# Split weight panels kept in DRAM and loaded back, and two PSUM banks that go through a panel half by half

## The chip, the cores and the metric

The kernel runs on one NeuronCore of a Trainium2 chip, in one launch. The metric is the device time of that launch in microseconds (us); lower is better. Three runs of the kernel before took 3841.34, 3851.86 and 3855.9 us; their median, 3851.86 us, is the time to compare with.

## The reference, cut to what matters

Two sequences go through one layer: a prompt of 256 tokens and a sample of 2048, each token a row of 1024 numbers. All arithmetic is float32.

```python
h = _rmsnorm(x, prm['norm_mix'][l])
p = h @ prm['w_in'][l]                     # 1024 -> 3504 columns
...                                        # three token mixers: GLA, RWKV-7, SSD, each in both directions
mix = jnp.concatenate([o_gla, o_rwkv, o_ssd], axis=-1)
x = x + mix @ prm['w_out'][l]              # 1024 -> 1024
h = _rmsnorm(x, prm['norm_ffn'][l])
x = x + (jax.nn.silu(h @ prm['ffn_gate'][l]) * (h @ prm['ffn_up'][l])) @ prm['ffn_down'][l]   # 2816 wide
```

The four projections are the dense work. `w_in` is used for 5 groups of tokens (the prompt's 256 and four times 512 of the sample), `w_out` for 9 blocks of 256 tokens, and the FFN weights for the same 5 groups.

## The kernel before, in words

**Split products.** A float32 product is made of three matmuls in the float32r form: each operand is the sum of a rounded part (hi) and the rest (lo), and hi times hi, hi times lo and lo times hi are added up in one PSUM bank (`acc3`, line 372: for every 128 rows k of the weights three matmuls). The activations are split when they are made (tiles `hT`, `mix`, and `b9`, `b9x`, the slots of the FFN's inner activations).

**Panels.** Weights come in panels of 256 columns (`panel`, line 281). A panel of 1024 rows has two halves of four k-blocks. For each pair of k-blocks a raw tile `wr` of 256 KB is loaded on SyncE's queue (line 293; 4 buffers, one whole panel), ScalarE copies it to `wh`, which rounds it (line 295), and VectorE subtracts to get `wl` (line 296; in the input projection GpSimd does every second of these). `wh` and `wl` have two buffers of one half each. So a panel costs four loads, four ScalarE copies and four subtractions each time it is used, and a half can be filled only after the matmuls have left the half that lay in its buffer. A panel has two outputs of 24 matmuls or, for 512 tokens with the tokens as output rows, four: in `in_chan` (line 382) and the FFN's gate and up two outputs of 128 columns by 512 tokens, in `tok` (line 395: `in_tok`, `out_proj`) two or four outputs of 128 tokens by 256 columns. Each output goes through both halves before the next begins, so the first half of the panel is left when three quarters of it are done (with four outputs, seven eighths), the second half at its end.

**PSUM.** Dense outputs take turns on the two banks of pool `d`; in the sample's output projection and the FFN (`dense(wide=True)`, line 144) a third one, `g`, joins them. `evac` (line 378) copies an output to a tile `ev`, on ScalarE and VectorE in turn.

**Stages.** Passes over the sequence interleave mixers and dense work. First the prompt's input projection (14 panels), then that of the sample's four groups (11, 14, 14, 14 panels, and at the end the 3 panels that the first group had left out: `in_gates`, line 439), each beside the forward mixers of the blocks before (`pass_a`, line 967). Then backwards: for each block of 256 tokens the backward mixers (`pass_b`, line 978) and the output projection (`out_proj`, line 1023, 4 panels), interleaved with the FFN of the groups already done (`ffn`, line 1039). The last group's FFN runs alone. The prompt's output projection comes early, beside the second group of the sample.

**Order.** The framework orders each engine's instructions before the run, by the order in the program, with priorities and by a simulated time line; each engine then works through its own list and waits on semaphores. A DMA is issued by the queue of its engine in that order too: SyncE's queue has the loads of panels, most of the mixers' loads and the stores of `ev`; ScalarE's the mixers' stores. An instruction that waits holds up all that stands behind it on its engine.

Of the kernel before, what the change touches and what calls it, by code (L numbers as in the profile page):

```python
# [8 lines left out]
F32 = mybir.dt.float32  # L9
F32R = mybir.dt.float32r  # L10
# [8 lines left out]
P = 128  # L19
# [50 lines left out]
class Encoder:  # L70
    def __init__(self, ctx, tc, ins, y_prompt, y_sample):
        self.ctx, self.tc, self.nc, self.ins = ctx, tc, tc.nc, ins
        self.Lp, self.Ls = ins["x_prompt"].shape[1], ins["x_sample"].shape[1]
        self.NT = self.Lp + self.Ls
        self.NB = self.NT // TB
        self.yp, self.ys = y_prompt, y_sample
        self.flip, self.free, self.turn = 0, False, 0
        pool = lambda n, b, **k: ctx.enter_context(tc.tile_pool(name=n, bufs=b, **k))
        self.cp = pool("const", 1)
        self.wp = pool("weights", 2)  # L80
        self.hp = pool("dense", 1)
# [33 lines left out]
    def mm(self, out, lhsT, rhs, start=True, stop=True, tp=None, lax=False):  # L115
        self.nc.tensor.matmul(out, lhsT=lhsT, rhs=rhs, start=start, stop=stop, tile_position=tp, skip_group_check=lax)  # L116

    SLOT = {"av0": "b9", "av1": "b9x", "acc0": "b4a", "acc1": "b4b", "acc2": "b4c", "acc3": "b4d", "gate": "b4e",
            "ga": "b4a", "gb": "b4b", "NF": "b4d", "gP": "b4e", "gqxb": "b2b", "gsq": "b2a", "gth": "b2b", "qgb": "qg", "ggt": "gv",
            "sxd": "b2b", "sth": "b2a", "qsb": "qs", "sz": "sxs", "sC": "scb", "sdr": "scb",  # L120
# [157 lines left out]
        return self.ins["x_sample"][0, t:t + P, :], self.ys[0, t:t + P, :]  # L278


    def panel(self, srcs, kt, pool=0):
        n = sum(w for _, w in srcs)
        nc, out = self.nc, []
        for k0 in range(0, kt, 4):
            kn = min(4, kt - k0)
            hi = self.wp.tile([P, 4, 256], F32R, tag="wh", name="wh", bufs=2)
            lo = self.wp.tile([P, 4, 256], F32R, tag="wl", name="wl", bufs=2)
            for j in range(0, kn, 2):
                raw = self.wp.tile([P, 2, 256], F32, tag="wr", name="wr", bufs=4)
                o = 0  # L290
                for ap, w in srcs:
                    with nc.allow_non_contiguous_dma(reason="column panel"):
                        nc.sync.dma_start(out=raw[:, :, o:o + w], in_=ap[(k0 + j) * P:(k0 + j + 2) * P, :].rearrange("(k p) n -> p k n", p=P))
                    o += w
                self.copy(hi[:, j:j + 2, :n], raw[:, :, :n], "a")
                self.tt(lo[:, j:j + 2, :n], raw[:, :, :n], hi[:, j:j + 2, :n], ALU.subtract, nc.gpsimd if j == 2 and pool else None)
            out += [(hi[:, k], lo[:, k]) for k in range(kn)]
        return out

    def inv_rms(self, x, tag):  # L300
# [68 lines left out]
    def new_hT(self):  # L369
        return [self.hp.tile([P, KD, GS], F32R, tag=f"hT{i}", name=f"hT{i}") for i in range(2)]  # L370

    def acc3(self, ps, lhs, rhs, kt):

        for k in range(kt):
            for a, b in ((0, 0), (0, 1), (1, 0)):
                self.mm(ps, lhs(k, a), rhs(k, b), start=k == 0 and a + b == 0, stop=k == kt - 1 and a == 1)

    def evac(self, out, in_):
        self.flip += 1
# [2 lines left out]
    def in_chan(self, hT, t0, n, cols, dst):  # L382

        w = self.ins["w_in"][0]
        pan = self.panel([(w[:, o:o + c], c) for o, c in cols], KD, 1)
        c0 = 0
        for dram, idx, rows in dst:
            ps = self.ps(self.dps, "d")
            self.acc3(ps[:rows, :n], lambda k, a: pan[k][a][:, c0:c0 + rows], lambda k, a: hT[a][:, k, :n], KD)
            ev = self.hp.tile([P, GS], F32, tag="ev", name="ev", bufs=3)  # L390
            self.evac(ev[:rows, :n], ps[:rows, :n])
            self.nc.sync.dma_start(out=dram[:rows, idx, t0:t0 + n], in_=ev[:rows, :n])
            c0 += rows

    def tok(self, lhs, pan, i, kt, wide=True):

        ps = self.dense(wide)
        self.acc3(ps[:, :256], lambda k, a: lhs[a][:, k, i * P:(i + 1) * P], lambda k, a: pan[k][a], kt)
        return ps[:, :256]

    def in_tok(self, hT, t0, n, off, dst, d0):
        pan = self.panel([(self.ins["w_in"][0][:, off:off + 256], 256)], KD, 1)
        for i in range(n // P):
            ps = self.tok(hT, pan, i, KD, False)
            ev = self.hp.tile([P, GS], F32, tag="ev", name="ev", bufs=3)
            self.evac(ev[:, :256], ps)
            self.nc.sync.dma_start(out=dst[t0 + i * P:t0 + (i + 1) * P, d0:d0 + 256], in_=ev[:, :256])

    def normed(self, t0, n, gain, src, rs=None):
        hT = self.new_hT()  # L410
# [612 lines left out]
    def out_proj(self, b, mix):  # L1023
        nc, t0 = self.nc, b * TB
        ss = [self.hp.tile([P, 4], F32, tag="so", name="so", bufs=4) for _ in range(2)]
        for c in range(4):
            cs = slice(256 * c, 256 * c + 256)
            pan = self.panel([(self.ins["w_out"][0][:, cs], 256)], KD)
            for i in range(2):
                x = self.hp.tile([P, 256], F32, tag="ev", name="xo", bufs=3)  # L1030
                nc.sync.dma_start(out=x[:], in_=self.xrow(t0 + i * P)[0][:, cs])
                self.tt(x[:], self.tok(mix, pan, i, KD, t0 >= self.Lp), x[:], ALU.add)
                nc.scalar.dma_start(out=self.d_x2[t0 + i * P:t0 + (i + 1) * P, cs], in_=x[:])
                self.square(ss[i], c, x[:])
        for i in range(2):
            self.rs2[t0 + i * P] = self.inv_rms4(ss[i], "rn", self.rn[:, t0 // P + i:t0 // P + i + 1])


    def ffn(self, t0, n, after=None, inside=False):
# [16 lines left out]
        for fn in [2] + [4] * ((FT - 2) // 4):  # L1056
            if not inside:
                av = [self.m([P, 4, GS], f"av{i}", F32R) for i in range(2)]
            for f in range(0, fn, 2):
                cs = slice((f0 + f) * P, (f0 + f + 2) * P)  # L1060
                if inside:
                    gate = self.hp.tile([P, 2, n], F32, tag="ev", name="gate", bufs=3)
                else:
                    gate = self.m([P, 2, GS], "gate")
                for name in ("ffn_gate", "ffn_up"):
                    pan = self.panel([(ins[name][0][:, cs], 256)], KD)
                    for j in range(2):
                        ps = self.dense(not inside)
                        self.acc3(ps[:, :n], lambda k, a: pan[k][a][:, j * P:(j + 1) * P], lambda k, a: hT[a][:, k, :n], KD)
                        if name == "ffn_gate":  # L1070
                            self.act(gate[:, j, :n], ps[:, :n], AF.Tanh, scale=0.5)
                            self.stt(gate[:, j, :n], gate[:, j, :n], 1.0, ps[:, :n], ALU.add, ALU.mult)
                        else:
                            self.stt(gate[:, j, :n], ps[:, :n], 0.5, gate[:, j, :n], ALU.mult, ALU.mult)
                            self.copy(av[0][:, f + j, :n], gate[:, j, :n], "a")
                            self.tt(av[1][:, f + j, :n], gate[:, j, :n], av[0][:, f + j, :n], ALU.subtract)
            for c in range(4):
                half = None
                if f0 + fn == FT and after and c < after[1] // P:
                    with self.tc.high_priority(offset=3000):  # L1080
                        t = after[0] + c * P
                        ready = self.ready.get(after[0]) or self.ready.setdefault(after[0], self.new_hT())
                        half = self.norm_T(self.d_x2[t:t + P, :], g, ready, c, self.rs2[t])
                cs = slice(256 * c, 256 * c + 256)
                pan = self.panel([(ins["ffn_down"][0][f0 * P:(f0 + fn) * P, cs], 256)], fn)
                for i in range(nt):
                    self.tt(acc[i][:, c], self.tok(av, pan, i, fn, not inside), acc[i][:, c], ALU.add)
# [121 lines left out]
```

## Time and profile before

| | |
|---|---|
| median of three runs | 3851.86 us |
| profiled execution | 3852.02 us |
| its span, first to last instruction | 3850.2 us |
| TensorE busy | 3607.3 us, 94% |
| VectorE busy | 2453.1 us, 64% |
| ScalarE busy | 1459.3 us, 38% |
| GpSimd busy | 560.5 us, 15% |
| mean granted TensorE clock | 0.963 of 2.4 GHz |
| DMA | 486.5 MB, 126 GB/s |

PE is TensorE's matmul side, PEld its weight loads, DVE VectorE, ACT ScalarE, POOL GpSimd, SP SyncE (a queue of DMAs here). A matmul's duration overlaps that of the next one, so that a busy PE need not be at its peak: what a stream of matmuls costs is the distance of their starts. L116 is line 116 of the kernel. The chain that ended last is followed back from the last instruction, at each step to what released it or to the instruction before it on its engine.

### The profile page before, as it was taken

The numbers are of one execution on the slowest core, as the hardware profiler recorded it, in microseconds if no ns is written. First come the engines' busy times: TensorE is split into PE (matmuls) and PEld (weight loads), VectorE is DVE, ScalarE is ACT, GpSimd is POOL, SyncE is SP. The second block draws the span as 40 slices with busy tenths as digits, with TensorE's granted clock in tenths as the row PEclk, the third lists the DMA queues.
The fourth block names the chain that finished last, engine by engine and source line by source line (L and its number), as shares of the span: only waits on it lengthen the run. The fifth ranks groups of instructions, "written<-read, shape, count | busy, mean of one in ns | idle before, by whom it ended". The sixth has DMA issues, their size and how long they took to land.

```text
span 3850.2 us, 75004 instructions
## 1 busy us (share of the span) xinstructions
PE 3607.3 (94%) x29534; PEld 3022.0 (78%) x29534; DVE 2453.1 (64%) x5551; ACT 1459.3 (38%) x3228; POOL 560.5 (15%) x564
## 2 busy tenths in 40 slices
PE   6898889899989879899989999999999999999998
PEld 6777676667767667788878888888888888888887
DVE  5943486784893788876766565565654765645444
ACT  4533244544453455443432323323233332333222
POOL 2321113332332333110000000000000000000000
PEclk9899899999989988998999999999999999999999
DMA  6444242434324423455543434434343442434232
GB/s 177 157 140 123 88 149 96 126 98 134 124 92 127 134 94 112 150 165 162 169 151 122 128 119 131 135 128 136 102 146 103 146 131 83 147 105 137 93 99 93
DMA packets 430192, 486.50 MB, mean 126 GB/s; under 512 B 49344, under 2 KB 389456, under 8 KB 428688
## 3 DMA queue, kind: packets, MB, share of 16 engines
q1 hardware_dynamic: 390720, 422.40, 35.5%
q10 hardware_dynamic: 38112, 55.65, 4.1%
q8 instruction: 232, 3.80, 0.4%
q0 software_dynamic: 1008, 3.67, 0.3%
q14 instruction: 120, 0.98, 0.1%
HBM read 395.42 MB, written 86.18 MB: 125 GB/s over the span
## 4 chain that ended last, share of the span: by engine, by line
PE 75%; DVE 13%; DMA 6%; ACT 3%; issue 2%; POOL 0%; ACTq 0%; SPq 0%; DVEq 0%; POOLq 0%
PE d L116 47%; PE g L116 15%; PE s L116 5%; PE a L116 3%; PE c L116 3%; DVE mix L102 3%; DMA mix<-d_xb 1%; DVE wl L92 1%; DMA x<-d_x 1%; DVE mix L92 1%; PE d L362 1%; DVE x L102 1%; DMA b<-d_rk 1%; DMA x<-in_x_sample 1%; ACT wh L109 0%
## 5 line engine op out<-in xcount | busy, mean ns | idle before, releaser
L116 PE MATMUL d<-hT,wh 128*128 128x512 f32 (+3 forms) x4384 | 1272.5, 374 | 12.8 <-ACT wh L109 4.6
L109 ACT ACTIVATE wh<-wr 128x512 fp32r<-128x512 f32 (+1 forms) x1084 | 624.6, 621 | 987.2 <-PE d L116 573.1
L116 PEld LDWEIGHTS d<-hT,wh 128*128 128x128 f32 (+1 forms) x4384 | 788.9, 191 | 162.5 <-issue 10.2
L92 DVE TENSOR_TENSOR wl<-wr,wh 128x512 fp32r<-128x512 f32 x944 | 651.8, 718 | 338.0 <-ACT wh L109 322.9
L116 PE MATMUL d<-hT,wl 128*128 128x512 f32 (+2 forms) x2192 | 811.9, 374 | 24.3 <-DVE wl L92 24.1
L116 PEld LDWEIGHTS d<-hT,wl 128*128 128x128 f32 (+1 forms) x2192 | 416.9, 191 | 103.6 <-DVE wl L92 29.1
L116 PE MATMUL g<-hT,wh 128*128 128x512 f32 x896 | 285.1, 394 | 0.1
L116 PE MATMUL d<-wh,hT 128*128 128x256 f32 x1216 | 259.0, 303 | 14.6 <-ACT wh L109 8.2
L116 PE MATMUL d<-wh,b 128*128 128x256 f32 x928 | 266.3, 289 | 4.7 <-DVE b4d L92 3.2
L92 POOL TENSOR_TENSOR wl<-wr,wh 128x512 fp32r<-128x512 f32 (+1 forms) x140 | 198.3, 1420 | 485.6 <-ACT wh L109 365.7
L116 PE MATMUL d<-wl,b 128*128 128x256 f32 x928 | 260.2, 282 | 0.0
L116 PE MATMUL d<-wh,b9x 128*128 128x256 f32 x928 | 257.9, 281 | 0.0
L116 PEld LDWEIGHTS d<-wh,hT 128*128 128x128 f32 x1216 | 206.3, 202 | 26.5 <-ACT wh L109 10.0
L116 PEld LDWEIGHTS g<-hT,wh 128*128 128x128 f32 x896 | 166.6, 188 | 35.3 <-issue 0.7
L116 PE MATMUL d<-wl,hT 128*128 128x256 f32 x608 | 182.5, 302 | 9.5 <-DVE wl L92 9.5
L116 PEld LDWEIGHTS d<-wh,b 128*128 128x128 f32 x928 | 174.1, 188 | 12.3 <-DVE b4d L92 3.6
L116 PE MATMUL d<-wh,mix 128*128 128x256 f32 x832 | 168.8, 292 | 8.3 <-ACT mix L109 5.5
L116 PE MATMUL g<-hT,wl 128*128 128x512 f32 x448 | 175.5, 392 | 0.0
L116 PEld LDWEIGHTS d<-wl,b 128*128 128x128 f32 x928 | 174.7, 189 | 0.7 <-issue 0.3
L116 PEld LDWEIGHTS d<-wh,b9x 128*128 128x128 f32 x928 | 174.5, 189 | 0.5
L102 DVE SCALAR_TENSOR_TENSOR mix<-mix,cwh,mix 128x256 f32<-128x256 f32 x288 | 140.3, 539 | 18.3 <-ACT mix L105 18.2
L116 PEld LDWEIGHTS d<-wh,mix 128*128 128x128 f32 x832 | 135.8, 195 | 11.7 <-ACT mix L109 5.8
(384 smaller groups left out, 6220.9 us busy)
## 6 DMA issues: line engine op xcount, KB each, us to landing
wr<-in_w_in SPq DMA_DIRECT2D x260, 256.0 KB, 3.4
wr<-in_ffn_gate SPq DMA_DIRECT2D x220, 256.0 KB, 2.9
wr<-in_ffn_up SPq DMA_DIRECT2D x220, 256.0 KB, 2.9
wr<-in_ffn_down SPq DMA_DIRECT2D x220, 256.0 KB, 2.8
wr<-in_w_out SPq DMA_DIRECT2D x144, 256.0 KB, 3.3
x<-in_x_sample SPq DMA_DIRECT2D x20, 512.0 KB, 3.5
x<-d_x SPq DMA_DIRECT2D x20, 512.0 KB, 3.9
q_s<-qs ACTq DMA_DIRECT2D x18, 520.0 KB, 3.1
```

Source lines behind the costliest of these rows:

```text
L92: (eng or self.nc.vector).tensor_tensor(out=out, in0=a, in1=b, op=op)
L102: (eng or self.nc.vector).scalar_tensor_tensor(out=out, in0=a, scalar=s, in1=b, op0=op0, op1=op1)
L109: self.nc.scalar.activation(out=out, in_=in_, func=AF.Copy)
L116: self.nc.tensor.matmul(out, lhsT=lhsT, rhs=rhs, start=start, stop=stop, tile_position=tp, skip_group_check=lax)
L362: self.nc.tensor.transpose(ps[:, k * P:(k + 1) * P], h[:, (4 * q + k) * P:(4 * q + k + 1) * P], self.c["ident"])
```

## The change

A panel now has a name, and the kernel counts its uses. The 14 panels of `w_in` are split as before in their first use (the prompt) and in their second; after the second, ScalarE's queue also writes the four split halves (two `wh`, two `wl`, 512 KB each) to DRAM. From the third use on no raw tile is loaded, copied or subtracted: SyncE's queue loads the split halves into `wh` and `wl`, four DMAs of 512 KB in place of four of 256 KB. For `w_out` the first use writes and the other 8 load. The FFN's panels are split at each use, as before. The two buffers of `wh` and `wl` get names of their own, and a list tells which is free first.

`acc3` now takes several outputs (`jobs`) and goes through the panel half by half: all outputs take the first half, then all take the second, so that as many PSUM banks are in use at once. With four outputs (`in_tok` with 512 tokens) the first pair takes the halves in the order 0, 1, the second pair in the order 1, 0, and the next panel's first half goes to the buffer that is free first. `ffn_down`'s panels of four k-blocks are one half, and are used one output at a time as before.

```diff
+        self.uses, self.kept, self.slots = {}, {}, [0, 1]
...
+    KEPT = {"w_in": 2, "w_out": 1}
...
-    def panel(self, srcs, kt, pool=0):
+    def panel(self, name, srcs, kt, pool=0, snake=False):
         n = sum(w for _, w in srcs)
-        nc, out = self.nc, []
+        nc, out, slots = self.nc, [], []
+        use = self.uses[name] = self.uses.get(name, 0) + 1
+        kept = self.kept.get(name)
+        keep = kept is None and use == self.KEPT.get(name[0], 0)
+        if keep:
+            kept = self.kept[name] = self.dr.tile([2, P, kt, n], F32, name=f"d_w{len(self.kept)}", tag=f"d_w{len(self.kept)}")
         for k0 in range(0, kt, 4):
             kn = min(4, kt - k0)
-            hi = self.wp.tile([P, 4, 256], F32R, tag="wh", name="wh", bufs=2)
-            lo = self.wp.tile([P, 4, 256], F32R, tag="wl", name="wl", bufs=2)
-            for j in range(0, kn, 2):
...
+            slot = self.slots.pop(0)
+            slots.append(slot)
+            hi = self.wp.tile([P, 4, 256], F32R, tag=f"wh{slot}", name="wh", bufs=1)
+            lo = self.wp.tile([P, 4, 256], F32R, tag=f"wl{slot}", name="wl", bufs=1)
+            parts = [(hi[:, :kn, :n], 0), (lo[:, :kn, :n], 1)]
+            if kept is not None and not keep:
+                for t, i in parts:
+                    nc.sync.dma_start(out=t.bitcast(F32), in_=kept[i, :, k0:k0 + kn])
+            else:
+                for j in range(0, kn, 2):
...
+                if keep:
+                    for t, i in parts:
+                        nc.scalar.dma_start(out=kept[i, :, k0:k0 + kn], in_=t.bitcast(F32))
+            out.append([(hi[:, k], lo[:, k]) for k in range(kn)])
+        self.slots += slots[::-1] if snake else slots
         return out
...
-    def acc3(self, ps, lhs, rhs, kt):
-        for k in range(kt):
-            for a, b in ((0, 0), (0, 1), (1, 0)):
-                self.mm(ps, lhs(k, a), rhs(k, b), start=k == 0 and a + b == 0, stop=k == kt - 1 and a == 1)
+    def acc3(self, jobs, pan, kt, order=(0, 1)):
+        order = order[:1] if len(pan) == 1 else order
+        for n, q in enumerate(order):
+            for ps, lhs, rhs in jobs:
+                for j, w in enumerate(pan[q]):
+                    for a, b in ((0, 0), (0, 1), (1, 0)):
+                        self.mm(ps, lhs(4 * q + j, a, w), rhs(4 * q + j, b, w), start=n == 0 and j == 0 and a + b == 0,
+                                stop=n == len(order) - 1 and j == len(pan[q]) - 1 and a == 1)
...
     def in_tok(self, hT, t0, n, off, dst, d0):
-        pan = self.panel([(self.ins["w_in"][0][:, off:off + 256], 256)], KD, 1)
-        for i in range(n // P):
-            ps = self.tok(hT, pan, i, KD, False)
...
+        pan = self.panel(("w_in", off), [(self.ins["w_in"][0][:, off:off + 256], 256)], KD, 1, snake=n == GS)
+        for i0 in range(0, n // P, 2):
+            for i, ps in enumerate(self.tok(hT, pan, (i0, i0 + 1), KD, False, (0, 1) if i0 == 0 else (1, 0)), i0):
...
-            pan = self.panel([(self.ins["w_out"][0][:, cs], 256)], KD)
-            for i in range(2):
+            pan = self.panel(("w_out", c), [(self.ins["w_out"][0][:, cs], 256)], KD)
+            for i, ps in enumerate(self.tok(mix, pan, (0, 1), KD, t0 >= self.Lp)):
...
-                self.tt(x[:], self.tok(mix, pan, i, KD, t0 >= self.Lp), x[:], ALU.add)
+                self.tt(x[:], ps, x[:], ALU.add)
...
-                    pan = self.panel([(ins[name][0][:, cs], 256)], KD)
-                    for j in range(2):
-                        ps = self.dense(not inside)
-                        self.acc3(ps[:, :n], lambda k, a: pan[k][a][:, j * P:(j + 1) * P], lambda k, a: hT[a][:, k, :n], KD)
+                    pan = self.panel((name, f0 + f), [(ins[name][0][:, cs], 256)], KD)
+                    jobs = [(self.dense(not inside)[:, :n], lambda k, a, w, j=j: w[a][:, j * P:(j + 1) * P],
+                             lambda k, a, w: hT[a][:, k, :n]) for j in range(2)]
+                    self.acc3(jobs, pan, KD)
```

## Rows read from the trace of the kernel before

**Rows 1.** The page's head: busy time of each engine.
```profile
PE 3607.3 (94%) x29534; PEld 3022.0 (78%) x29534; DVE 2453.1 (64%) x5551; ACT 1459.3 (38%) x3228; POOL 560.5 (15%) x564
```
**Rows 2.** Stages: length, busy PE, PEld, DVE, ACT, POOL, clock, DMA share, GB/s.
```profile
115.00:400.00 285.00, 261.17 (x2194) 202.50 (x2193) 161.57 (x343) 110.72 (x260) 74.97 (x68) 0.95 0.45 139
400.00:1560.00 1160.00, 1032.90 (x9098) 801.44 (x9098) 843.75 (x1844) 532.80 (x1219) 342.51 (x346) 0.92 0.36 114
1560.00:1960.00 400.00, 375.08 (x4294) 341.26 (x4292) 299.02 (x737) 167.02 (x385) 35.94 (x40) 0.96 0.54 170
1960.00:3330.00 1370.00, 1354.97 (x10509) 1158.62 (x10509) 831.65 (x1932) 442.14 (x939) 70.53 (x70) 1.00 0.39 125
```
**Rows 3.** The chain of waits by line: 400 to 1560, 1560 to 1960, 1960 to 3330.
```profile
by line: PE d L116 30.2%; DVE mix L102 7.5%; PE a L116 6.9%; PE s L116 4.6%; DMA mix<-d_xb 4.6%; issue 4.6%; PE g L116 3.6%; PE c L116 2.8%; DVE mix L92 2.0%; DVE wl L92 2.0%; DMA b<-d_rk 1.8%; DVE b L129 1.5%; ACT mix L105 1.3%; ACT b4a L1
by line: PE d L116 53.0%; PE s L116 10.9%; PE c L116 7.1%; PE g L116 5.9%; issue 2.7%; PE a L116 2.3%; DVE wl L92 1.8%; DMA sxs<-d_z 1.8%; DVE srs L102 1.1%; PE s L593 1.1%; DMA d_x<-xo 0.9%; DMA x<-d_x 0.9%; DMA b<-d_gl 0.6%; DVE b9x L92 0
by line: PE d L116 53.4%; PE g L116 25.9%; PE s L116 6.0%; PE c L116 3.3%; PE a L116 1.9%; DMA x<-d_x 1.6%; DMA qg<-q_g 1.0%; DVE wl L92 0.9%; PE d L362 0.8%; issue 0.8%; DMA wr<-in_w_out 0.6%; PE a L1019 0.4%; DMA wr<-in_ffn_gate 0.4%; PE 
```
**Rows 4.** The splits: duration ns least/median/most.
```profile
L109 ACT ACTIVATE wh<-wr x1084: 480/620/667, 14.0 to 3827.4; 128x512 fp32r<-128x512 f32 x178, 128x352 fp32r<-128x352 f32 x3
L92 DVE TENSOR_TENSOR wl<-wr,wh x944: 514/686/1796, 15.8 to 3828.2; 128x512 fp32r<-128x512 f32 x188, 128x352 fp32r<-128x352 f32 x1
L92 POOL TENSOR_TENSOR wl<-wr,wh x140: 927/1316/3867, 15.2 to 1506.1; 128x512 fp32r<-128x512 f32 x130, 128x352 fp32r<-128x352 f32 x10
```
**Rows 5.** Who waited for what: us in total, times, longest.
```profile
PE d L116 <- DVE wl L92: 33.9, 22, 4.0
PE d L116 <- ACT wh L109: 13.1, 11, 5.0
PE d L116 <- DVE ev L113: 9.6, 5, 4.0
ACT wh L109 <- PE d L116: 573.1, 258, 8.7
```
**Rows 6.** Pieces of the chain: start, us, matmuls; 512 columns, then 256.
```profile
3338.32 10.88 PE d L116 x48
2131.20 5.62 PE d L116 x46
```
**Rows 7.** Matmuls on `mix` in the first, third and last of eight sample blocks.
```profile
L116 PE MATMUL d<-wh,mix x96: 276/281/582, 1788.2 to 1820.4; 128*128 128x256 f32 x96
...
L116 PE MATMUL d<-wh,mix x96: 277/281/387, 2105.5 to 2136.5; 128*128 128x256 f32 x96
...
L116 PE MATMUL d<-wh,mix x80: 276/281/290, 3302.9 to 3327.6; 128*128 128x256 f32 x80
L116 PE MATMUL g<-wh,mix x48: 277/281/387, 3301.5 to 3327.0; 128*128 128x256 f32 x48
```
**Rows 8.** DMA issues: count, KB each, median us from issue to landing.
```profile
wr<-in_w_out SPq DMA_DIRECT2D x144, 256.0 KB, 3.3
x<-in_x_sample SPq DMA_DIRECT2D x20, 512.0 KB, 3.5
```
**Rows 9.** Four loads of 512 KB in a row: SyncE's time line, then landings.
```profile
1958.20 0.34 SPq L353 DMA_DIRECT2D x<-d_x  x1
1958.59 0.42 SPq L1054 DMA_DIRECT2D b4a<-d_x  x1
1959.11 0.38 SPq L353 DMA_DIRECT2D x<-d_x  x1
1959.54 0.42 SPq L1054 DMA_DIRECT2D b4b<-d_x  x1
...
b4a<-d_x SPq DMA_DIRECT2D x1, 512.0 KB, 4.5
b4b<-d_x SPq DMA_DIRECT2D x1, 512.0 KB, 6.2
```
**Rows 10.** ScalarE's DMA queue: packets, MB, share of 16 engines' span.
```profile
q10 hardware_dynamic: 38112, 55.65, 4.1%
```

More of the change, by code (lines that the diff above doesn't have):

```diff
@@ L284, in panel @@
         for k0 in range(0, kt, 4):
             kn = min(4, kt - k0)
-            hi = self.wp.tile([P, 4, 256], F32R, tag="wh", name="wh", bufs=2)
-            lo = self.wp.tile([P, 4, 256], F32R, tag="wl", name="wl", bufs=2)
-            for j in range(0, kn, 2):
[L289 to L296, printed above, removed]
@@ L297, in panel @@
-            out += [(hi[:, k], lo[:, k]) for k in range(kn)]
+            slot = self.slots.pop(0)
[8 more added lines that the diff above has]
+                for j in range(0, kn, 2):
+                    raw = self.wp.tile([P, 2, 256], F32, tag="wr", name="wr", bufs=4)
+                    o = 0
+                    for ap, w in srcs:
+                        with nc.allow_non_contiguous_dma(reason="column panel"):
+                            nc.sync.dma_start(out=raw[:, :, o:o + w], in_=ap[(k0 + j) * P:(k0 + j + 2) * P, :].rearrange("(k p) n -> p k n", p=P))
+                        o += w
+                    self.copy(hi[:, j:j + 2, :n], raw[:, :, :n], "a")
+                    self.tt(lo[:, j:j + 2, :n], raw[:, :, :n], hi[:, j:j + 2, :n], ALU.subtract, nc.gpsimd if j == 2 and pool else None)
+                if keep:
+                    for t, i in parts:
+                        nc.scalar.dma_start(out=kept[i, :, k0:k0 + kn], in_=t.bitcast(F32))
@@ L384, in in_chan @@
         w = self.ins["w_in"][0]
-        pan = self.panel([(w[:, o:o + c], c) for o, c in cols], KD, 1)
-        c0 = 0
+        pan = self.panel(("w_in", cols[0][0]), [(w[:, o:o + c], c) for o, c in cols], KD, 1)
+        c0, jobs = 0, []
         for dram, idx, rows in dst:
             ps = self.ps(self.dps, "d")
-            self.acc3(ps[:rows, :n], lambda k, a: pan[k][a][:, c0:c0 + rows], lambda k, a: hT[a][:, k, :n], KD)
+            jobs.append((ps[:rows, :n], lambda k, a, w, c0=c0, rows=rows: w[a][:, c0:c0 + rows], lambda k, a, w: hT[a][:, k, :n]))
+            c0 += rows
@@ L390, in in_chan @@
+        self.acc3(jobs, pan, KD)
+        for (ps, _, _), (dram, idx, rows) in zip(jobs, dst):
             ev = self.hp.tile([P, GS], F32, tag="ev", name="ev", bufs=3)
-            self.evac(ev[:rows, :n], ps[:rows, :n])
+            self.evac(ev[:rows, :n], ps)
             self.nc.sync.dma_start(out=dram[:rows, idx, t0:t0 + n], in_=ev[:rows, :n])
[L393 to L399, printed above, removed]
@@ L401, in in_tok, with tok @@
-    def in_tok(self, hT, t0, n, off, dst, d0):
-        pan = self.panel([(self.ins["w_in"][0][:, off:off + 256], 256)], KD, 1)
-        for i in range(n // P):
-            ps = self.tok(hT, pan, i, KD, False)
-            ev = self.hp.tile([P, GS], F32, tag="ev", name="ev", bufs=3)
-            self.evac(ev[:, :256], ps)
-            self.nc.sync.dma_start(out=dst[t0 + i * P:t0 + (i + 1) * P, d0:d0 + 256], in_=ev[:, :256])
+    def tok(self, lhs, pan, tiles, kt, wide=True, order=(0, 1)):
+        jobs = [(self.dense(wide)[:, :256], lambda k, a, w, i=i: lhs[a][:, k, i * P:(i + 1) * P], lambda k, a, w: w[a]) for i in tiles]
+        self.acc3(jobs, pan, kt, order)
+        return [j[0] for j in jobs]
@@ new lines, in in_tok @@
+    def in_tok(self, hT, t0, n, off, dst, d0):
+        pan = self.panel(("w_in", off), [(self.ins["w_in"][0][:, off:off + 256], 256)], KD, 1, snake=n == GS)
+        for i0 in range(0, n // P, 2):
+            for i, ps in enumerate(self.tok(hT, pan, (i0, i0 + 1), KD, False, (0, 1) if i0 == 0 else (1, 0)), i0):
+                ev = self.hp.tile([P, GS], F32, tag="ev", name="ev", bufs=3)
+                self.evac(ev[:, :256], ps)
+                self.nc.sync.dma_start(out=dst[t0 + i * P:t0 + (i + 1) * P, d0:d0 + 256], in_=ev[:, :256])
@@ L1084, in ffn @@
                 cs = slice(256 * c, 256 * c + 256)
-                pan = self.panel([(ins["ffn_down"][0][f0 * P:(f0 + fn) * P, cs], 256)], fn)
+                pan = self.panel(("ffn_down", f0, c), [(ins["ffn_down"][0][f0 * P:(f0 + fn) * P, cs], 256)], fn)
                 for i in range(nt):
-                    self.tt(acc[i][:, c], self.tok(av, pan, i, fn, not inside), acc[i][:, c], ALU.add)
+                    self.tt(acc[i][:, c], self.tok(av, pan, (i,), fn, not inside)[0], acc[i][:, c], ALU.add)
                     if f0 + fn == FT:
```

8 lines of the change are left out of this document (5 added, 3 removed).

## The prediction, made before the changed kernel was run

> **What bounds the kernel now.** I read the head of the page first: TensorE is busy 94% of the span, VectorE 64%, ScalarE 38% [rows 1]. That is an average, so the stages come next [rows 2]. In 1960 to 3330 TensorE is busy 1355 of 1370 us at full clock: little can be gained there by anything that is not TensorE's own work. In 400 to 1560, the input projection of the sample beside the forward mixers, it is busy 1033 of 1160 us at a granted clock of 0.92, with VectorE at 844 us. There the chain of waits alternates between TensorE, VectorE and the mixers' loads [rows 3]: the matmul entries in its row add up to 48%. Only then do I ask what panels cost. The subtraction of `wl` is 2.0% of that chain, 1.8% of the one from 1560 to 1960 and 0.9% of the one from 1960 to 3330 [rows 3], that is 23, 7 and 12 us. In all, dense matmuls waited 33.9 us for `wl` and 13.1 us for `wh` [rows 5]. The loads of raw tiles are early: what ScalarE's copies wait for is a buffer that TensorE has not left yet, 573 us in 258 waits [rows 5], not a DMA. So the panels' price today is some 50 us of waits, out of 3850.
>
> **What is removed.** Of 70 panels of `w_in` the last 42 are loaded split, of 36 of `w_out` the last 32. Each had four copies and four subtractions. ScalarE loses 74 x 4 = 296 copies of 0.62 us, 184 us; VectorE 84 + 128 = 212 subtractions of 0.69 us, 146 us; GpSimd 84 of 1.3 us, 110 us [rows 4]. Of this only 84 subtractions, 58 us of VectorE, and 168 copies, 104 us of ScalarE, lie in 400 to 1560, where these engines are on the path; that is 7% of what VectorE does there. The other subtractions and copies lie in the output projection, beside a full TensorE.
>
> **What is added: loads between release and use.** Before, the load was done ahead, and between the release of a half and its use stood a copy and a subtraction, 0.62 + 0.69 us for the first two k-blocks. Now the whole load stands there, two DMAs of 512 KB. A load of that size lands 3.5 us after its issue, a raw one of 256 KB after 3.3 [rows 8]. Four such loads in a row bound a pair and a whole panel: the second was issued 0.39 us after the first and landed 4.5 us later, 4.9 us in all, and the fourth landed 7.5 us after the first was issued [rows 9]. I take 4.9 us for a half. Against it stands the time in which the other half is used: 24 matmuls. With 512 columns at 10.88/48 = 0.227 us that is 5.4 us, with 256 columns at 5.62/46 = 0.122 us it is 2.9 us [rows 6].
>
> In `in_chan` 5.4 us cover 4.9. In the 9 loaded `in_tok` panels (four outputs) the first buffer is freed 24 matmuls, 2.9 us, before the panel's end: 2 us late, 18 us over all; mixer matmuls are plenty there, so I take half, +9 (from 0 to 18).
>
> In the output projection, a half comes every (2.9 + 4.9)/2 us with two buffers, a panel every 7.8 us, a block of four panels every 31.3 us. TensorE needs 4 x 48 x 0.122 = 23.4 us. Today the blocks last 32.2, 31.0 and, where hardly any mixer work is mixed in, 26.1 us [rows 7]; with some 30 us as the typical one, six of them are mixer matmuls. If these go into the gaps, a block loses 1 to 2 us, if they don't, 7.9. I take +2.5: nearer to the first, since the order is made with the loads in view. Eight blocks: two in 1560 to 1960, +5, six later, +15 (from 0 to 63 in all).
>
> The Trainium skill (DMA: Bandwidth & Descriptors, § Anatomy of one DMA) fits a DMA of GpSimd's path as 2.0 us and its bytes over 436 GB/s. By it, as an estimate, 1 MB takes 4.4 us, a panel comes every 7.3 us and a block every 29, which would make the output projection free; the trace has 4.9 us for two halves of that size, and the sum goes by it.
>
> **The bytes.** 42 panels bring 1 MB more each, 44 MB; ScalarE's queue moved 55.65 MB in 4.1% of the span, 158 us, 352 GB/s [rows 10], so they take 125 us of all DMA engines, and the share in 400 to 1560 goes from 0.36 to some 0.47. The mixers' own loads stand for 4.6% and 1.8% of that chain [rows 3], 74 us; slower by 5 to 10% they cost +5 (from 0 to 15). SyncE's queue waits for buffers as it did before, now for TensorE to leave them rather than for a subtraction; behind it stand the mixers' loads and the stores of `ev`.
>
> **The stores.** 18 panels, 72 stores of 512 KB, 44 of them in 115 to 400, 23 MB or 66 us at 352 GB/s: a DMA share from 0.45 to 0.68 there [rows 2]. ScalarE, busy 111 of 285 us, waits at each second one for a GpSimd subtraction of 1.3 us, and evacuations queue behind it; TensorE is the bound in that stage and the raw tiles are early. Zero, from -5 to +10.
>
> **Half by half.** A half's buffer is now freed at half of the panel, not at three quarters: the slack of a split goes from 12 matmuls to 24. That helps the FFN and the first two uses. But both banks are open from the panel's start: the first output is done at 3/4 instead of 1/2, so its evacuation has 12 matmuls rather than 24 before its bank is wanted again where there are two banks; with 256 columns that is 1.5 us. Waits for `ev` on VectorE are 9.6 us now [rows 5]; I let them grow by 5 in 400 to 1560 and by 2 later (from 0 to 20). In the last FFN, from 3330 on, 48 matmuls follow each other at 0.227 us: nothing to gain or lose.
>
> **The sum**, against the profiled execution (3852.0 us, of which the span is 3850.2; the median of the runs is 3851.9, the same):
> - to 400: more slack for the splits against the stores: -2.
> - 400 to 1560: the 23 us of `wl` on the chain go, +9 for `in_tok`, +5 for slower loads, +5 for banks: -4. If VectorE were the bound throughout, -58.
> - 1560 to 1960: -7 + 5 + 2 = 0.
> - 1960 to 3330: half of the 12 us of `wl` and half of the 8 us (0.6%) of raw loads of `w_out` on the chain [rows 3] go, the rest is taken by what was late just behind them: -10, +15 for six blocks: +5.
> - Together about -1; with some relief of ScalarE's queue in 400 to 1560, which the chain shows only in small pieces, -6: **3846 us, no change that can be told** (0.5%, 19 us, is about what a measurement of this kernel can tell).
>
> **The rivals.**
> 1. *The loads are hidden and the queues freed* (chance 0.30). The order places mixer work into every gap of the output projection and ScalarE and VectorE, 7% lighter, let the mixers' chain run ahead. Then all of `wl` on the chain (23 + 7 + 12), 8 us of raw loads and 5 to 30 us of VectorE's relief go: -50 to -75, near 3795. For it: VectorE at 73% in 400 to 1560, the long waits of ScalarE for buffers. Against it: where TensorE is full, only idle time can be won, 15 us in 1960 to 3330. The skill's fit of a DMA above belongs to this case.
> 2. *The output projection runs at the pace of its loads* (0.22). The point that decides: whether a half is there within the 2.9 us of the other half and the mixer matmuls beside it. If the load takes nearer 7.5 us than 4.9 (the DMA share in a block, 2.1 MB in 7.8 us, is already 270 GB/s before the mixers' loads), a panel takes (2.9 + 7.5) = 10.4 us, a block 42: +11 on each of eight, and gaps remain even with the mixers. With -15 of the gains left: +50 to +75, near 3905. For it: TensorE full, two buffers, no load ahead. Against it: the other loads can wait.
> 3. *Nothing moves* (0.08). The chain's 2% of `wl` is taken over by another wait of the same length at once: 3852.
> My forecast, with its own range of 3825 to 3865, has 0.40.
>
> **How the numbers follow.** Faster by over 0.5% (under 3833): most of rival 1 and a quarter of the forecast, 0.28 + 0.10 = 0.38. Slower (over 3871): rival 2, and a few hundredths of the forecast: 0.20 + 0.04 = 0.24. The rest, 0.38, in between. The range takes in most of rivals 1 and 2, 3788 to 3905.
>
> **What would show it.** The chain from 400 to 1560 without `wl` but with a few per cent of DMA into `wh` or `wl`; blocks of the output projection of 31 to 34 us, the last one, with no mixers, longer than its 26.1 by 5 us; VectorE some 146 us and ScalarE some 184 us less busy; the halves landing 4.5 to 5.5 us after issue; the FFN alone unchanged. Blocks of 38 us or more make rival 2 right, blocks under 30 us and a stage of 400 to 1560 shorter by 40 us rival 1.

## The result, and the profile after

The changed kernel took 3887.8 us (median of four runs, 3886.3 to 3894.6) against 3846.6 us for the kernel before: a ratio of 1.0115, with a 95% interval of 1.0096 to 1.0135. It is 41 us slower, where no change that can be told was forecast (-6 us). The profiled execution took 3894.6 us, its span 3892.8.

The head of the page of the changed kernel, which answers to [rows 1]:

```profile
PE 3608.9 (93%) x29534; PEld 3041.5 (78%) x29534; DVE 2289.7 (59%) x5339; ACT 1302.4 (33%) x2932; POOL 451.6 (12%) x480
```

TensorE has the same 29534 matmuls. VectorE lost 2453.1 - 2289.7 = 163 us, ScalarE 157, GpSimd 109: the work that was to go has gone. By stage, with the columns of [rows 2], the stages' ends moved to about where the same work ends:

```profile
115.00:390.00 275.00, 253.07 (x2144) 196.62 (x2143) 148.60 (x335) 105.74 (x250) 70.09 (x62) 0.95 0.69 227
390.00:1500.00 1110.00, 1000.33 (x8742) 779.33 (x8742) 737.64 (x1711) 433.28 (x1021) 223.51 (x253) 0.93 0.51 167
1500.00:1960.00 460.00, 416.37 (x4711) 372.31 (x4713) 308.65 (x753) 166.76 (x392) 47.11 (x53) 0.92 0.54 171
1960.00:3372.00 1412.00, 1352.05 (x10436) 1171.68 (x10437) 769.53 (x1832) 387.04 (x837) 71.04 (x70) 0.98 0.44 139
```

In the last of these TensorE is idle for 60 us where it had been idle for 15, and its clock is no longer full. What it waits for is in the chain of waits of that stretch (one row, as in [rows 3]), and in the waits of TensorE over the whole span (columns as in [rows 5]):

```profile
by line: PE d L117 49.8%; PE g L117 25.1%; DMA wh<-d_w 9.2%; PE s L117 4.2%; PE c L117 3.0%; PE a L117 1.9%; DMA qg<-q_g 1.4%; issue 0.8%; DMA x<-d_x 0.7%; PE d L384 0.5%; PE a L1048 0.4%; PE s L622 0.3%; POOL b2b L93 0.3%; DVE wl L93 0.3%;
```
```profile
PE d L117 <- DMA wh<-d_w: 52.5, 26, 5.6
...
PE g L117 <- DMA wh<-d_w: 15.5, 13, 2.6
PE d L117 <- ACT ev L110: 14.4, 7, 4.4
PE d L117 <- DVE ev L114: 13.5, 5, 6.4
...
PE d L117 <- DVE wl L93: 8.3, 9, 2.3
...
PE d L117 <- ACT wh L110: 4.4, 3, 2.8
```

A wait that was not there before, a DMA into `wh`, is 9.2% of 1412 us, 130 us of the chain, where the subtraction of `wl` had been 0.9%. (Some of the matmuls of a chain can stand beside such a load, so this is not yet the loss.) The place is the output projection. Its blocks, with matmuls on `mix` as in [rows 7], the first, third and last of the eight:

```profile
L117 PE MATMUL d<-wh,mix x96: 276/282/582, 1771.5 to 1812.0; 128*128 128x256 f32 x96
...
L117 PE MATMUL d<-wh,mix x96: 276/281/533, 2105.6 to 2142.8; 128*128 128x256 f32 x96
...
L117 PE MATMUL d<-wh,mix x80: 276/282/581, 3333.1 to 3371.2; 128*128 128x256 f32 x80
L117 PE MATMUL g<-wh,mix x48: 276/282/582, 3331.7 to 3368.7; 128*128 128x256 f32 x48
```

They last 40.5, 37.2 and 39.5 us, against 32.2, 31.0 and 26.1. Over all eight, from the first to the last start, I find 319 us of blocks after and 240 before: +79 us. Of these, 18 come back in the stretches between the blocks and 1 behind the last, since mixer work that used to be done beside the FFN is now done in the gaps, and 17 had been gained before the first of them: 79 - 18 - 1 - 17 = +43, the difference of the spans (3892.8 - 3850.2). The fifth block shows where the mixer work went, before and then after (columns as in [rows 2]): TensorE has 254 matmuls in it, then 416.

```profile
2610.00:2639.00 29.00, 29.00 (x254) 26.88 (x253) 16.14 (x30) 12.94 (x31) 0.00 (x0) 1.00 0.56 176
```
```profile
2625.00:2662.00 37.00, 30.66 (x416) 28.47 (x416) 10.47 (x24) 7.48 (x26) 0.00 (x0) 1.00 0.79 252
```

The last block, which has no mixer work beside it, shows the cycle undisturbed. First SyncE's queue with the loads of halves as they are issued (those at 3339, 3349 and 3359 fill the same buffer, the one at 3342 the other), then TensorE's long waits, then how long the two dozens of matmuls of a half took (pieces of the chain, as in [rows 6]):

```profile
3339.44 0.32 SPq L304 DMA_DIRECT2D wl<-d_w  x1
3339.85 0.38 SPq L304 DMA_DIRECT2D wh<-d_w  x1
...
3342.34 0.32 SPq L304 DMA_DIRECT2D wl<-d_w  x1
3342.76 0.38 SPq L304 DMA_DIRECT2D wh<-d_w  x1
...
3349.62 0.32 SPq L304 DMA_DIRECT2D wl<-d_w  x1
3350.03 0.38 SPq L304 DMA_DIRECT2D wh<-d_w  x1
...
3359.88 0.32 SPq L304 DMA_DIRECT2D wl<-d_w  x1
```
```profile
3345.28 0.58 PE L117 MATMUL d<-wh,mix 128*128 128x256 f32 x1 [2.85 <-DMA wh<-d_w]
3355.57 0.58 PE L117 MATMUL d<-wh,mix 128*128 128x256 f32 x1 [3.04 <-DMA wh<-d_w]
```
```profile
3345.28 2.93 PE d L117 x12
3348.21 1.50 PE g L117 x12
```

A buffer is free at 3339.44, its half is there and the first matmul starts at 3345.28, 5.84 us later; the half is used until 3349.62, 4.34 us. That cycle takes 10.18 us, the next one (from 3349.62 to 3359.88) 10.26. A cycle of both buffers is one panel, four panels are a block. The 24 matmuls of a half, 2.9 us at full clock, take 4.34 here, because the clock has fallen: the first dozen takes 2.93 us, the second 1.50. The same stretch of the kernel before and after (columns as in [rows 2]; the clock is the one before the DMA share):

```profile
3301.00:3328.00 27.00, 25.65 (x206) 24.60 (x205) 16.54 (x36) 12.99 (x29) 0.00 (x0) 1.00 0.57 182
```
```profile
3332.00:3372.00 40.00, 29.74 (x196) 28.43 (x195) 4.94 (x11) 5.03 (x17) 0.00 (x0) 0.83 0.70 237
```

A mean of 0.83 means that a third of the block ran at 1.2 GHz, after waits of some 3 us. The Trainium skill (TensorE: Matmul & The Clock Gate, § HAM oscillation) tells of bursts of matmuls between waits for DMAs that fall back to half clock; the trace agrees with 0.83 against 1.00.

### The profile page after: what moved, and what is told of

Its sections match the earlier page's. It is cut to its first block, busy times and chain, and to the rows that moved or that the text cites. A ratio compares the mean times of both kernels' runs of the same rounds, so it can differ in the third digit from the quotient of the medians.

```text
span 3892.8 us, 74207 instructions
## 1 busy us (share of the span) xinstructions
PE 3608.9 (93%) x29534; PEld 3041.5 (78%) x29534; DVE 2289.7 (59%) x5339; ACT 1302.4 (33%) x2932; POOL 451.6 (12%) x480
## 4 chain that ended last, share of the span: by engine, by line
PE 53%; DMA 7%; DVE 4%; issue 1%; ACT 1%; POOL 0%; SPq 0%; ACTq 0%; DVEq 0%; POOLq 0%
PE d L117 32%; PE g L117 14%; DMA wh<-d_w 4%; PE s L117 3%; PE c L117 2%; PE a L117 2%; DMA qg<-q_g 1%; DVE wl L93 0%; DMA x<-d_x 0%; PE d L384 0%; DMA mix<-d_xb 0%; DVE b9x L103 0%; DMA x<-in_x_sample 0%; DVE mix L93 0%; PE a L1048 0%
## 5 line engine op out<-in xcount | busy, mean ns | idle before, releaser
L117 PE MATMUL d<-hT,wl 128*128 128x512 f32 (+3 forms) x2192 | 812.8, 373 | 6.3 <-DVE wl L93 6.2
L110 ACT ACTIVATE wh<-wr 128x512 fp32r<-128x512 f32 x788 | 455.8, 623 | 916.2 <-PE d L117 544.3
L93 DVE TENSOR_TENSOR wl<-wr,wh 128x512 fp32r<-128x512 f32 (+1 forms) x732 | 498.4, 711 | 397.4 <-ACT wh L110 379.4
L117 PE MATMUL d<-wh,mix 128*128 128x256 f32 x832 | 184.3, 310 | 49.1 <-DMA wh<-d_w 38.2
L117 PEld LDWEIGHTS d<-wh,mix 128*128 128x128 f32 x832 | 148.8, 211 | 55.8 <-DMA wh<-d_w 38.9
L103 DVE SCALAR_TENSOR_TENSOR mix<-mix,cwh,mix 128x256 f32<-128x256 f32 x288 | 124.7, 488 | 43.1 <-ACT mix L106 38.2
L117 PE MATMUL g<-wh,b 128*128 128x256 f32 x480 | 139.8, 291 | 2.3 <-DVE b4a L93 2.0
```

The source lines that it names most:

```text
L93: (eng or self.nc.vector).tensor_tensor(out=out, in0=a, in1=b, op=op)
L103: (eng or self.nc.vector).scalar_tensor_tensor(out=out, in0=a, scalar=s, in1=b, op0=op0, op1=op1)
L110: self.nc.scalar.activation(out=out, in_=in_, func=AF.Copy)
```

## The experiments

All ran beside the kernel before on the same chip; its medians were 3844 to 3849 us.

**1. The order alone.**

```diff
-    KEPT = {"w_in": 2, "w_out": 1}
+    KEPT = {}
```

> The half-by-half order alone; every panel is split at each use, nothing is written or loaded split. Theory A (the loads of w_out's halves stand between release and use and leave TensorE idle; this costs all of the loss): 3835 to 3855 us, output projection blocks of 26 to 34 us as before, VectorE busy as before (2453 us). Theory B (two banks held open are what costs, above all in the prompt's FFN with its two banks, which took some 35 us longer): 3875 us or more, with the stretch between the end of the input projection and the first sample block of the output projection as long as in the changed kernel (275 us against 237 before).

3837.5 us, ratio 0.9975 (0.9965 to 0.9986). The order does not lose time; this version gains 10 us. Theory B falls. Of theory A the time holds, the blocks only in part: three of the eight last longer than 34 us (34.6, 37.7 and 39.8). And the edit did less than its text says. The framework orders the instructions anew, and in the last block (26.2 us, 26.1 before) TensorE goes through the outputs in the same order in the kernel before and in this run. The block's first pieces of the chain in either:

```profile
3301.66 1.41 PE g L116 x12
3303.07 2.95 PE d L116 x25
```
```profile
3288.05 1.41 PE g L117 x12
3289.46 2.95 PE d L117 x25
```

After 12 of its 24 matmuls the output in `g` gives way to those in `d`. So there an output did not go through both halves before the next began in the kernel before either, although its program has it so.

**2 and 3. The loads of one weight alone.**

```diff
-    KEPT = {"w_in": 2, "w_out": 1}
+    KEPT = {"w_in": 2}       # the third run: {"w_out": 1}
```

> The change with w_out split at each use; w_in is kept and loaded. Theory A: the forward part keeps its gain of some 50 us, the eight blocks are 26 to 34 us again (they are 83 us longer in the changed kernel, of which the stretches between them give some back): 3795 to 3820 us. Theory B: 3860 us or more, since the order is still there.

> The change with w_in split at each use; w_out is kept and loaded. Theory A: no gain in the forward part, blocks of 36 to 48 us: 3900 to 3940 us, the slowest of the four. Theory B: 3860 to 3890 us, no slower than the changed kernel.

With `w_in` alone 3835.2 us, 0.9967 (0.9953 to 0.9980): the right side, but 15 us short of theory A's range. With `w_out` alone 3910.0 us, 1.0166 (1.0147 to 1.0186). Theory A holds for that run, with blocks of 36 to 44 us. So the loads of `w_out` cost 72 us without those of `w_in` (3910.0 against 3837.5) and 53 with them (3887.8 against 3835.2), and `w_in`'s are worth 2 us in the one pair and 22 in the other: each version gets another order of all its instructions, and differences of 10 to 20 us between neighbours are not one edit's alone. The traces part the two. From the first start of the first sample block to the end of the span, with the same matmuls still to do, the kernel before takes 2062 us, runs 1 and 2 take 2068 and 2072, run 3 and the changed kernel 2116 and 2121: there the loads of `w_out` cost 48 us in the one pair and 49 in the other. The profiled executions of the two pairs lie 69 and 60 us apart; the other 22 and 11 us are lost before that block, when only the first panel of these loads has been issued, and nothing here shows why. The last block of the run with `w_in` alone is back at 28.4 us (first to last start, 3281.4 to 3309.8; after the change 39.5), though three of the eight are longer than theory A has them (35.8, 36.4 and 39.9):

```profile
L117 PE MATMUL d<-wh,mix x80: 276/281/415, 3282.9 to 3309.8; 128*128 128x256 f32 x80
L117 PE MATMUL g<-wh,mix x48: 277/282/582, 3281.4 to 3309.2; 128*128 128x256 f32 x48
```

**4. The loads with the old order.** `acc3` takes one output through both halves, then the next, and the buffers are used in turn.

```diff
-        for n, q in enumerate(order):
-            for ps, lhs, rhs in jobs:
+        for ps, lhs, rhs in jobs:
+            for q in range(len(pan)):
...
-        pan = self.panel(("w_in", off), [(self.ins["w_in"][0][:, off:off + 256], 256)], KD, 1, snake=n == GS)
+        pan = self.panel(("w_in", off), [(self.ins["w_in"][0][:, off:off + 256], 256)], KD, 1)
```

> The loads with the old order: one output goes through both halves before the next begins, and the buffers are used in turn. A half is then released 12 matmuls before it is wanted rather than 24. Theory A: blocks longer still, by up to 1.5 us a half, 45 to 52 us each, 3910 to 3960 us. Theory B: the banks are free early again: 3840 to 3870 us.

3911.6 us, 1.0158 (1.0134 to 1.0182): in theory A's range, but for another reason. Theory A's longer blocks were a miss: the eight sum to 307 us, with the new order to 319. But the run does not test that, since it does not have the old order there. The framework came out with the same order for the last block as in the changed kernel: both outputs through one half, then both through the other. Its pieces of the chain, to be compared with the two dozens above (the old order would have 24 of one output in a row):

```profile
3368.03 2.25 PE d L117 x12
3370.28 2.39 PE g L117 x12
```

So the loads of one buffer, issued at 3362.18, 3372.57 and 3382.78 us, have a cycle of 10.2 to 10.4 us as in the changed kernel, and whether the order of the two outputs would set the pace is not shown. The loss against the changed kernel lies in the forward part: the first sample block starts at 1803 us, there at 1771, 32 us later, of which the shorter blocks give 12 back.

**5 and 6. Where did the forward part's gain go?** The input projection's last output is copied out at 1555.6 us in the kernel before and at 1500.0 in the changed one, 55 us earlier, but the first sample block starts only 17 us earlier (1771.5 against 1788.2). I suspected the prompt's FFN, whose two banks are open at once, and gave it the old order; run 6 gives that order to the whole FFN and to `out_proj`. Both load `w_in` alone.

```diff
-    def acc3(self, jobs, pan, kt, order=(0, 1)):
+    def acc3(self, jobs, pan, kt, order=(0, 1), seq=False):
+        if seq and len(jobs) > 1:
+            for job in jobs:
+                self.acc3([job], pan, kt)
+            return
...
-                    self.acc3(jobs, pan, KD)
+                    self.acc3(jobs, pan, KD, seq=inside)    # run 6: seq=True, here and in out_proj
```

> The version with w_in alone loaded, and the old order of outputs in the prompt's FFN (the only FFN with two banks). In the runs so far the forward part ended 50 us earlier with the new order, and some 30 of these were gone by the first sample block. Theory 1 (the two open banks of the prompt's FFN cost these 30): 3800 to 3815 us. Theory 2 (nothing was lost there: mixer work that the forward part no longer did was done there instead, TensorE being full in both): 3830 to 3845 us, as with the new order.

> As the run before, with the old order in the whole FFN and in the output projection too, so that only the input projection goes half by half. Theory 1: 3795 to 3815 us. Theory 2: within 10 us of the run before; if the half-by-half order helps the splits of the FFN, up to 10 us slower.

3821.2 us, 0.9933 (0.9918 to 0.9948), the fastest of all versions, and 3828.7 us, 0.9955 (0.9940 to 0.9969), within 10 us of it, as theory 2 had it. Neither theory's range holds the first. Its 14 us against run 2 are not won where the edit is. The gate and up matmuls of the prompt's FFN, in run 2 and then in run 5:

```profile
L117 PE MATMUL d<-hT,wh x704: 274/283/681, 1510.2 to 1873.3; 128*128 128x256 f32 x176
```
```profile
L117 PE MATMUL d<-hT,wh x704: 277/283/681, 1509.4 to 1875.8; 128*128 128x256 f32 x176
```

They take 363 us with both banks open and 366 with the old order, and the first sample block starts at 1760.7 and 1763.3. What run 5 gains, it gains behind them, where the two programs are the same, so the cause stays open; it may be one more of the differences that come with a new order of all instructions. (The same edit is worth 5 us between runs 1 and 9 and 11 between runs 7 and 11.) So the 38 us that the forward part had lost on the way (55 - 17) are not the banks' either. Theory 2 is right there, and the counts of matmuls show it. The span up to the end of the input projection and up to the first sample block, of the kernel before and then of the changed one:

```profile
0.00:1552.00 1552.00, 1370.97 (x11800) 1076.44 (x11800) 1062.69 (x2332) 691.97 (x1592) 451.11 (x452) 0.93 0.40 122
0.00:1788.00 1788.00, 1585.65 (x14359) 1268.35 (x14360) 1240.19 (x2741) 785.67 (x1795) 476.50 (x480) 0.93 0.41 128
```
```profile
0.00:1497.00 1497.00, 1335.15 (x11466) 1053.05 (x11466) 952.91 (x2207) 590.11 (x1388) 330.99 (x354) 0.94 0.55 180
0.00:1771.00 1771.00, 1584.12 (x14354) 1269.36 (x14356) 1151.17 (x2652) 696.77 (x1623) 367.57 (x396) 0.93 0.54 175
```

The changed kernel has done 334 matmuls less when its input projection is through (all of them mixers'; the dense ones are the same), and as many as the kernel before at the first block. A landmark of one kind of work that comes earlier is no gain when other work has been put off past it. The gain that is left at the block, 17 us, is the forward part's own; with the order alone it is 21 (1766.9), with `w_in` loaded too 28 (1760.7).

**7. A buffer more.** Of the eight halves of a block the third and the sixth go into the four raw tiles, which the output projection no longer uses.

```diff
+            if kept is not None and not keep and name[0] == "w_out":
+                self.turn3 = getattr(self, "turn3", -1) + 1
+                if self.turn3 % 8 in (2, 5):
+                    third = [[self.wp.tile([P, 2, 256], F32, tag="wr", name="wr", bufs=4) for _ in range(2)] for _ in range(2)]
...
+                            nc.sync.dma_start(out=third[i][j][:, :, :n], in_=kept[i, :, k0 + 2 * j:k0 + 2 * j + 2])
```

> The full change, but of the eight halves of an output projection block the third and the sixth are loaded into the four raw tiles, which nothing else uses then: a third buffer, so that a load can stand ahead. Theory A1 (the loss is the load's latency between release and use): a half has three uses of 2.9 us in its cycle instead of two, 5.7 us of load fit, blocks of 27 to 33 us, 3830 to 3850 us. Theory A2 (the loss is the bytes: 2.1 MB a panel are more than the DMA engines bring in the 5.9 us that TensorE needs): blocks of 33 to 38 us, 3865 to 3890 us.

3843.1 us, 0.9996 (0.9981 to 1.0010), in theory A1's range. With the same bytes, 45 us are back; from the first sample block to the end it takes 2070 us, as without the loads. The loads themselves are no faster (median landing of `wh`, in the changed kernel and then here, from 1700 to 3400 us):

```profile
wh<-d_w SPq DMA_DIRECT2D x64, 512.0 KB, 5.7
```
```profile
wh<-d_w SPq DMA_DIRECT2D x48, 512.0 KB, 5.7
```

The last block lasts 29.2 us, its DMA engines 90% busy:

```profile
L117 PE MATMUL d<-wh,mix x56: 277/281/553, 3283.6 to 3311.4; 128*128 128x256 f32 x56
L117 PE MATMUL g<-wh,mix x40: 276/281/387, 3282.2 to 3309.9; 128*128 128x256 f32 x40
...
L117 PE MATMUL d<-wr,mix x36: 277/281/290, 3285.1 to 3303.9; 128*128 128x256 f32 x36
```
```profile
3286.00:3312.00 26.00, 21.78 (x165) 21.07 (x164) 3.69 (x8) 4.43 (x15) 0.00 (x0) 0.93 0.90 294
```

Theory A1 holds: what costs is that the load stands between the release of a half and its use. (Three of the eight blocks are longer than the 33 us that it allows. And the two halves of a block that go into the raw tiles come as four loads of 256 KB each, not as two of 512.) Whether the bytes, with 90%, are the next bound was not tried.

**8. Half the bytes.** Each load of `w_out` brings two of the four k-blocks and the matmuls use them twice, so the kernel leaves out half of the output projection's sums.

```diff
-                    nc.sync.dma_start(out=t.bitcast(F32), in_=kept[i, :, k0:k0 + kn])
+                    m = 2 if name[0] == "w_out" else kn
+                    nc.sync.dma_start(out=t[:, :m].bitcast(F32), in_=kept[i, :, k0:k0 + m])
...
+            out.append([(hi[:, k % m], lo[:, k % m]) for k in range(kn)])
```

> The full change, but each load of w_out brings two of the four k-blocks and the matmuls use these two twice (half of the contraction of the output projection is left out, the matmul work is the same). Theory A1 (latency): a load of 256 KB lands some 1.5 to 2 us earlier than one of 512 KB, a panel comes 2 to 4 us earlier, blocks of 27 to 33 us, 3845 to 3865 us. Theory A2 (bytes): with half of them the DMA engines are no bound, blocks of 26 to 30 us, 3830 to 3845 us.

3843.2 us, 0.9984 (0.9971 to 0.9997), blocks of 30 to 40 us: the time is in theory A2's range and just short of A1's, the blocks are longer than either has them. The loads land after 3.5 and 3.7 us (median) instead of 4.5 and 5.7 in the output projection of the changed kernel:

```profile
wl<-d_w SPq DMA_DIRECT2D x64, 256.0 KB, 3.5
wh<-d_w SPq DMA_DIRECT2D x64, 256.0 KB, 3.7
```

1 to 2 us less latency bring the time to where a third buffer does. This run alone does not part the two theories, since half the bytes shorten both; run 7 does.

**9. The fastest version without its loads**: run 5 with `KEPT = {}`.

> The fastest version so far (w_in loaded, the prompt's FFN in the old order, 3821 us) without any load: every panel split at each use. Theory L (loading w_in is worth something, since VectorE, ScalarE and GpSimd lose the splits): 3835 to 3850 us. Theory N (its loads give back what the splits cost, as 3837.5 against 3835.2 us suggested): 3815 to 3828 us.

3832.1 us, 0.9966 (0.9953 to 0.9978), between the two ranges. The interval of run 5 (0.9918 to 0.9948) lies below it: the loads of `w_in` are worth some 11 us here. In the traces the gain stands already at the first sample block, which starts at 1779.0 us without the loads and at 1763.3 with them.

**10. Filling the gaps.**

```diff
+            if fill is not None and n:
+                for i in range(12):
+                    self.mm(jobs[i % 2][0], self.zero[:], fill[:, i % 4, 0:256], start=False, stop=False)
...
+        if fill is not None:
+            for i in range(12):
+                self.mm(jobs[i % 2][0], self.zero[:], fill[:, i % 4, 0:256], start=False, stop=i > 9)
```

> The full change, and in the sample's output projection 12 matmuls with a stationary operand of zeros after each half (1.5 us a half at 0.122 us each, 11.7 us a block, 94 us of added TensorE work in all; they add zeros to the two open outputs and need nothing that is loaded). They stand where TensorE would wait for the next half. Theory C (a good part of a block's length is that TensorE's clock falls to 1.2 GHz after the gaps: 63 us at half clock between 1960 us and the end of the last block against 14 before): the clock stays up, the last block falls from 39.5 to 34 to 37 us and the whole to 3865 to 3885 us in spite of the added work. Theory G (the gaps alone): the last block stays at 38 to 41 us, since the added work fits into its gaps of 3 us a panel, the others get longer by what mixer work is pushed out, 3890 to 3940 us.

3952.1 us, 1.0277 (1.0249 to 1.0305), slower than either theory had it. The clock stayed higher in the last block (0.96, not 0.83), which lasts 46 us all the same:

```profile
3384.00:3430.00 46.00, 38.59 (x291) 36.58 (x290) 10.53 (x27) 6.76 (x19) 0.00 (x0) 0.96 0.58 195
```

The added matmuls, 11 us of them, did not go into the gaps: by the distances of its matmuls TensorE waits some 12 us in the changed kernel's last block and 9 in this one. The longest of these waits (2.9 us) has its reason in SyncE's queue, where the loads of a half stand behind the load of an `xo` tile that waits for its buffer:

```profile
3414.06 0.33 SPq L1068 DMA_DIRECT2D xo<-in_x_sample  x1
3414.49 0.38 SPq L306 DMA_DIRECT2D wh<-d_w  x1
```

So this run moved the loads as well as the clock, and what the clock costs by itself stays open. From the cycle above it is 4.34 - 2.93 = 1.4 us of each 10.3 there. Over the eight blocks the traces have 63 us at half clock after the change and 5 before; as an estimate from that, the clock has at most half of 58, 29 us, of the 79.

**11. Can `w_out`'s loads pay at all?** Run 7 with the prompt's FFN in the old order.

> The full change with the third buffer and the old order in the prompt's FFN: can w_out's loads be made to pay once they stand ahead? If the old order there is worth the 14 us that it was without w_out's loads: 3825 to 3832 us. If the freed 92 us of VectorE and 79 us of ScalarE in the output projection help at all, below 3821 us.

3831.9 us, 0.9963 (0.9950 to 0.9976): as the first range had it; the second, below 3821 us, is missed. Even with a buffer more it is 11 us slower than run 5, which splits `w_out` each time.

## Why the prediction was wrong, step by step

- **The block of the output projection** is the step that failed: +2.5 us a block in the sum, +10 measured (319 - 240 over eight), of which the stretches between the blocks gave back 2. The sum had a load of 4.9 us and a use of 2.9, a panel every 7.8 us; the last block shows 5.84 and 4.34, a panel every 10.2. The load was sized from two loads in a row of which the second landed 4.5 us after its issue [rows 9]; in the last block the second of a pair, issued 0.41 us after the first, landed 5.5 us after its issue, 5.7 at the median of all blocks. Why later is not shown; loads and stores of 128 KB of the same block run beside it. The use: 2.9 us became 4.3, because the clock fell, which the sum had at nothing. The mixer work did go into the gaps, as the sum had it: the blocks with it are as long as the one without (40.5 and 37.2 against 39.5). But more went into them than the six us of mixer matmuls that a block had before, and this was taken out of the stretches between, where only 18 of the 79 us came back.
- **Rival 2**, which had 0.22, is what happened: blocks of 36 to 48 us, six of the eight over its sign of 38, paced by the loads, with the point that decides where it was put (a half not there within the 2.9 us of the other). Runs 1 to 3 show the price, 48 and 49 us from the first sample block on, run 7 its cause. That its panel of 10.4 us fits is partly luck: it took a load of 7.5 us and full clock, and the runs show a load nearer to 4.9 and a fallen clock.
- The Trainium skill's fit of a DMA (DMA: Bandwidth & Descriptors, § Anatomy of one DMA), given for GpSimd's path, from which the prediction's estimate has 1 MB there after 4.4 us and the output projection free, was further off than the rows: 5.84 us here, on SyncE's queue. The measurement decides.
- **The splits that went**: VectorE 163 us (146 forecast), ScalarE 157 (184), GpSimd 109 (110). That they were worth little was right: TensorE's waits for `wl` on `d` fell from 33.9 to 8.3 us and those for ScalarE's `wh` from 13.1 to 4.4, and the loads of `w_in` are worth 2, 11 and 22 us in three pairs.
- **The bytes and the stores**: the DMA shares of 0.69 up to 390 us and 0.51 up to 1500 are near the 0.68 and 0.47 forecast.
- **To 1560 us**: -6 forecast, -17 at the first sample block. Where it comes from is not settled: run 1, with the order alone, has -21 there, but run 3, with the same order, none (1788.7).
- **1960 to 3330**: +5 forecast. The stretch from 1960 to the last block's end went from 1368 to 1412 us, +44: the six blocks in it are 57 us longer, the stretches between them 13 shorter.
- **Half by half**: TensorE's waits for evacuations on `d`, the banks' price, had +7 in the sum; over the span they went from 9.6 to 13.5 us on VectorE and from 1.2 to 14.4 on ScalarE, +17. Whether that is the order's is not shown: the framework had mixed the outputs in the kernel before as well (run 1).
- **The last FFN**, forecast unchanged, is: 522 us from the last block's end (3850.2 - 3328) before, 521 after.

## What to carry to other kernels

A split or cast that is done again at each use is not saved by loading its result if the load then stands where the split stood: the raw load had run ahead in buffers of its own, and the finished half cannot. Compare the load's latency, from the release of a buffer to the first instruction that reads it, with the time in which the other buffers are used; if it is longer, give it a buffer more or leave it (run 7 against the change). Weigh where the saved work lies: `w_out`'s splits lay beside a full TensorE, and no run gained by their going, `w_in`'s beside a busy VectorE, worth 2 to 22 us. And where a framework orders the instructions, read the order from the trace before an experiment on it is believed: in the output projection the edit of run 4 changed the program's order and not TensorE's.

## What the runs showed of the hardware

Two loads of 512 KB issued 0.4 us apart landed 4.5 and 5.7 us after their issue at the median of 64 pairs, where the loads of `x` of that size took 3.5 in the kernel before [rows 8]; halved to 256 KB, 3.5 and 3.7. In a block of 40 us with four waits of 1.7 to 3.0 us for loads, mostly 48 matmuls apart, the granted clock was 0.83. And with two buffers TensorE waited for loads that kept the DMA engines 0.70 busy in that block, while with a third one the same loads ran at 0.90.
